# Gate products with the high and low parts of u side by side: wide matmuls, chained products, and a written order for three groups

## The chip, the cores and the metric

The kernel runs on one core of a Trainium2 chip. The time is device time in microseconds of one execution, taken as the median of several runs; the profile is of one execution more. Engines are named as in the profile: PE is TensorE (matmuls), PEld its weight loads, DVE is VectorE, ACT is ScalarE, POOL is GpSimd and SP is SyncE, which issues most of the loads.

## The reference, cut to what matters

One layer of a streaming encoder over 512 frames of 1024 channels: three branches read the normalised input `u`, each branch is projected to 1024 channels, and three sigmoid gates, computed from `u`, merge them.

```python
u = rmsnorm(h, g_mix)
proj = u @ w_in                    # queries, keys, values, ..., 3 gates of 1024 columns
y_gla = o_gla @ w_gla_o            # branch outputs, 512 -> 1024
y_fox = o_fox @ w_fox_o
y_mem = o_mem @ w_mem_o
gt = sigmoid(gates)
merged = gt[0] * y_gla + gt[1] * y_fox + gt[2] * y_mem
h = h + merged @ w_out
u2 = rmsnorm(h, g_ffn)
h = h + square(relu(u2 @ w_ff1)) @ w_ff2
return rmsnorm(h, g_final)
```

All is float32. The change is in the gate products of the memory and the GLA branch, with small moves in the front (where `u` is made) and in the projection by `w_out`.

## The kernel before, in words

**Precision by parts.** Each float32 operand is split into a high part (rounded to the matmul's fp32r format, a cast on ACT) and a low part (the remainder, a subtraction on DVE). A product is three matmuls: high by high, high by low, low by high (`mm3`, L169 to L172). Weights go through `split_w` (L156): the cast is L160, the subtraction L161. Weight tiles rotate through three buffers each for raw, high and low data.

**Gates.** The gate matrix of a branch is 1024 by 1024. It is worked in two groups of 512 output channels (`i` = 0, 1), and each group as a 2 by 2 block product with seven block products instead of eight. On the side of `u` the blocks are quarters (4 channel blocks of 128 by 256 frames) and four sums of quarters (`S1` to `S4`, L1037); `GATE` (L1039) says which of them each of the products 1 to 7 uses. On the side of the weights the sums are made in DRAM order by loads that accumulate: `total` and `other` are loaded (L1064, L1065), and `plus` (L1069, the DMA is L1071, on POOL's queue) adds further blocks to them in place, each time after the split that still needed the earlier sum.

`product` (L1085) computes one block product into one PSUM bank of 2 by 256 columns: 8 pairs of output block `a` and channel block `k`, three matmuls of 256 columns each, 24 in all. `take` (L1094) adds or copies the bank into the four quarters `c11`, `c12`, `c21`, `c22` of the gate (sums at L1080, copies at L1096 and L1101) and applies the sigmoid as a tanh (L1083) when a quarter is complete. `output` (L1118) makes one 128-channel tile of the branch's projection: 12 matmuls of 512 columns (`o_tile`). `merge` (L1125) multiplies gate and projection on DVE (L1127) and adds the result to `acc` on POOL (L1128); for the GLA groups it also splits half of `acc` into `mh`, `ml` (L1131, L1132), the input of the next projection.

There are four groups: memory 0 and 1, GLA 0 and 1. The first has its first two weight tiles ready and makes the sums `S2`, `S4` as it goes (`lefts_2`, L1049). In the three others the order on PE is: products 1 and 2, an output tile, product 5, an output tile, products 3, 6, 7, an output tile, product 4, an output tile.

**Order.** PE's order is as written. On the other engines instructions are put in an order by the framework's scheduler, except where a stretch is wrapped in `in_order` (L138), which chains DVE, ACT and SP in the order of the text, and where `issue_after` puts one instruction behind another. `next_sum` (L122) issues, with each weight cast, one more of the sums of feed-forward weights that are built in DRAM, on POOL's queue.

**Output projection.** `gN` (L184) over `w_out` in two columns of 512 (L1248, L1249). The first column takes the channels two blocks at a time and keeps four banks open; the second loads its four weight tiles first (two of them into own tiles `f0`, `f1`) and goes frame block by frame block. The first two feed-forward weight tiles are split into `f2`, `f3` at L1251.

**Front.** `mem_values` (matmuls at L404) yields 16 steps. Between them stand the sums of squares of x (matmuls at L430), their mean (L431), the power -1/2 on POOL (L432), a transpose that spreads it over partitions (L437), the scaling of x (L441) and the split into `uhi`, `ulo` (L444, L447). `lead_w` (cast L416, subtraction L417) splits weight tiles by hand. The first projection of u starts with the matmuls at L609.

PSUM has eight banks: four named `mm` (products, projections), four named `a` (output tiles, transposes).

## Time and profile before

| what | us |
|---|---|
| median of 3 runs (lowest to highest) | 810.16 (809.69 to 810.54) |
| the profiled execution | 811.06 |
| its span, first instruction to last | 809.3 |
| PE busy in the span | 800.1 |
| DVE, ACT, POOL busy | 595.6, 444.7, 108.0 |
| granted TensorE clock, mean | 0.997 |

Matmuls overlap in the profile, so the time of one matmul in a stream is read from the difference of two starts, not from its duration. The front runs to about 45 us of the span, the first gate group starts near 318, the three others lie between about 346 and 440, the output projection between 440 and 487, and the feed-forward part after it.

### The profile page before, as it was taken

What the parts mean: (1) busy time and instruction counts of PE and PEld (TensorE: products, weight loads), DVE (VectorE), ACT (ScalarE), POOL (GpSimd) and SP (SyncE); (2) the same over time, 40 slices, a digit from 0 to 9 for tenths busy, and PEclk for the clock granted to TensorE, in tenths of its full rate; (3) what the DMA queues carried; (4) which work ended last, traced back from release to release, by engine and by line L of the source; (5) the groups of instructions that cost most, each with busy time, mean ns of one, the idle gap of its engine ahead of it and who ended that gap; (6) DMA issues with size and microseconds to landing.
All of it is one profiled execution on the core that took longest, in us unless ns stands there. A gap on an engine that the chain in (4) does not pass through costs nothing.

```text
span 809.3 us, 12486 instructions
## 1 busy us (share of the span) xinstructions
PE 800.1 (99%) x4799; PEld 704.9 (87%) x4799; DVE 595.6 (74%) x917; ACT 444.7 (55%) x702; POOL 108.0 (13%) x136
## 2 busy tenths in 40 slices
PE   9999999999999999999999999999999999999996
PEld 7788888888888888999999879988998899889985
DVE  6878878456465677877567368897788778877897
ACT  7767555443344234444354347874676367647764
POOL 0001010101101111143144000011001100100011
PEclk9999999999999999999999999999999999999998
DMA  9355665788887867757758723898758966896544
GB/s 358 137 160 175 185 164 178 213 226 246 215 266 239 234 210 198 186 138 206 204 134 238 254 81 130 275 258 217 240 165 195 220 213 173 191 274 202 162 83 130
DMA packets 39628, 161.29 MB, mean 199 GB/s; under 512 B 4752, under 2 KB 5456, under 8 KB 37200
## 3 DMA queue, kind: packets, MB, share of 16 engines
q0 software_dynamic: 9776, 58.20, 34.3%
q1 hardware_dynamic: 28432, 98.34, 34.2%
q10 hardware_dynamic: 1360, 3.96, 1.5%
q8 instruction: 37, 0.61, 0.3%
q14 instruction: 23, 0.19, 0.1%
HBM read 158.35 MB, written 35.68 MB: 240 GB/s over the span
## 4 chain that ended last, share of the span: by engine, by line
PE 94%; DMA 2%; DVE 1%; ACT 1%; issue 0%; POOLq 0%; DVEq 0%; POOL 0%; ACTq 0%
PE mm L1272 20%; PE mm L170 16%; PE mm L171 16%; PE mm L172 16%; PE a L171 5%; PE a L170 5%; PE a L172 5%; DMA raw<-in_wst_dram 2%; PE mm L391 1%; PE a L404 1%; PE a L662 1%; PE a L700 1%; PE a L699 1%; PE a L302 1%; PE a L939 1%; PE mm L618 0%
## 5 line engine op out<-in xcount | busy, mean ns | idle before, releaser
L170 PE MATMUL mm<-uhi,whi 128*128 128x512 f32 (+1 forms) x336 | 119.7, 356 | 0.0
L161 DVE TENSOR_TENSOR wlo<-raw,whi 128x1024 fp32r<-128x1024 f32 x61 | 79.6, 1306 | 53.0 <-ACT whi L160 53.0
L172 PE MATMUL mm<-uhi,wlo 128*128 128x512 f32 (+1 forms) x336 | 117.5, 350 | 0.0
L171 PE MATMUL mm<-ulo,whi 128*128 128x512 f32 (+1 forms) x336 | 117.3, 349 | 0.0
L160 ACT CAST whi<-raw 128x1024 fp32r<-128x1024 f32 x61 | 64.1, 1052 | 84.2 <-PE mm L171 47.8
L1328 ACT CAST hi<-raw 128x1024 fp32r<-128x1024 f32 x52 | 54.4, 1049 | 41.1 <-PE mm L1272 29.5
L1330 DVE TENSOR_TENSOR lo<-raw,hi 128x1024 fp32r<-128x1024 f32 x52 | 63.4, 1223 | 15.7 <-ACT hi L1328 15.7
L170 PEld LDWEIGHTS mm<-uhi,whi 128*128 128x128 f32 x336 | 63.7, 190 | 9.3 <-issue 1.5
L172 PEld LDWEIGHTS mm<-uhi,wlo 128*128 128x128 f32 x336 | 63.6, 189 | 8.5
L171 PEld LDWEIGHTS mm<-ulo,whi 128*128 128x128 f32 x336 | 63.7, 190 | 7.5
L1272 PE MATMUL mm<-u2l,hi 128*128 128x256 f32 x240 | 66.1, 283 | 0.0
L1272 PE MATMUL mm<-u2h,hi 128*128 128x256 f32 x240 | 66.1, 283 | 0.0
L1272 PE MATMUL mm<-u2h,lo 128*128 128x256 f32 x240 | 61.1, 283 | 0.0
L1632 POOL DMA_DIRECT2D b<-in_wst_dram x30 | 25.6, 855 | 262.2 <-DVE lo L1330 136.0
L1272 PE MATMUL mm<-u2sh,hi 128*128 128x256 f32 x192 | 52.5, 283 | 0.0
L1272 PE MATMUL mm<-u2sl,hi 128*128 128x256 f32 x192 | 52.5, 283 | 0.0
L170 PE MATMUL mm<-hi,ch 128*128 128x512 f32 (+1 forms) x132 | 50.9, 386 | 0.0
L171 PE MATMUL mm<-lo,ch 128*128 128x512 f32 (+1 forms) x132 | 50.9, 386 | 0.0
L172 PE MATMUL mm<-hi,cl 128*128 128x512 f32 (+1 forms) x132 | 50.9, 386 | 0.0
L1272 PE MATMUL mm<-u2sh,lo 128*128 128x256 f32 x192 | 47.5, 283 | 0.0
L1272 PEld LDWEIGHTS mm<-u2h,hi 128*128 128x128 f32 x240 | 46.1, 192 | 0.1
L1272 PEld LDWEIGHTS mm<-u2l,hi 128*128 128x128 f32 x240 | 46.1, 192 | 0.1
(446 smaller groups left out, 2144.9 us busy)
## 6 DMA issues: line engine op xcount, KB each, us to landing
raw<-in_wst_dram SPq DMA_DIRECT2D x113, 512.0 KB
raw<-T SPq DMA_DIRECT2D x32, 512.0 KB
b<-in_wst_dram POOLq DMA_DIRECT2D x32, 512.0 KB, 5.5
T<-in_wst_dram POOLq DMA_DIRECT2D x12, 1024.0 KB, 9.0
b<-in_wst_dram SPq DMA_DIRECT2D x16, 512.0 KB
wb<-in_wst_dram POOLq DMA_DIRECT2D x15, 512.0 KB, 5.4
T<-in_wst_dram POOLq DMA_DIRECT2D x12, 512.0 KB, 6.0
wb<-in_wst_dram SPq DMA_DIRECT2D x8, 512.0 KB
```

Source lines behind the costliest of these rows:

```text
L160: cast = nc.scalar.copy(hi, raw)
L161: low_now[0] = nc.vector.tensor_tensor(lo, raw, f(hi), op=ALU.subtract).ins
L170: nc.tensor.matmul(ps, lh, rh, start=start, stop=False, skip_group_check=on)
L171: nc.tensor.matmul(ps, lh, rl, start=False, stop=False, skip_group_check=on)
L172: nc.tensor.matmul(ps, ll, rh, start=False, stop=stop, skip_group_check=on)
L302: nc.tensor.matmul(ps, wz[:, :P], wz, start=True, stop=True)
L391: nc.tensor.matmul(kps[h], w[:, h * P:(h + 1) * P], x[:, k, :], start=k == p == 0, stop=k == KT - 1 and p == 2)
L404: nc.tensor.matmul(ps, x[:, k, sl], w[low][:, kk, :], start=k == low == 0 and x is mxh, stop=k == KT - 1 and low == 1)
L1272: nc.tensor.matmul(ps[:, a, :], x[:, a, k, :], y[:, s, k, :], start=start, stop=stop, skip_group_check=go is not None)
L1328: nc.scalar.copy(hi, raw)
L1330: nc.vector.tensor_tensor(lo, raw, f(hi), op=ALU.subtract)
L1632: nc.gpsimd.dma_start(to[i], wst[index["B", q, i, x]], accum_op=ALU.add)
```

## The change

1. `u` is kept in one tile, high part and low part side by side (`uhl`), and so are the sums (`J1` to `J4`, `own_pair`). A new `product` uses this in three groups: with high weights one matmul reads 256 columns of the high and 256 of the low part and writes both halves of a bank (512 columns); with low weights a matmul of 256 columns goes to the first half. The eight wide ones come first, then the eight narrow ones. A value of the gate is then the sum of the two halves of a bank.
2. Products are chained: a product starts an accumulation (1, 2, 5) or adds to what the bank pair already holds. Products 1, 6, 7, 4 go into the pair `x` and 2, 5, 3 into `y`; the next group swaps the pairs. For this the four `mm` banks become two tiles of two banks (`banks_of`), and the sign of the sums `S2` and of product 6 is turned.
3. The three later groups become a class `Group` whose `run` writes out the order on DVE, ACT and SP (`in_order`). The first group keeps its products.
4. Front: one step of `mem_values` moves from before the sums of squares to after the power, two more go behind the split of u, and one low part of a weight tile waits for the power.
5. Output projection: the first column uses two `a` and two `mm` banks; its weight tiles after the first are split behind the last reads of the gates; the first feed-forward tiles are split behind the last split before them.

The diff, cut to its core:

```diff
-    uhi = up.tile([P, KT, S], F32R, tag="uhi", name="uhi")
-    ulo = up.tile([P, KT, S], F32R, tag="ulo", name="ulo")
+    uhl = up.tile([P, 2, KT, S], F32R, tag="uhl", name="uhl")
+    uhi, ulo = (uhl[:, i] for i in range(2))
...
-        run(islice(mv, 9))
-        lead_w(chunks[7], vraws[1])()
+        run(islice(mv, 8))
+        low = lead_w(chunks[7], vraws[1])
...
-        nc.gpsimd.tensor_tensor(rx, ms, mhalf[:, :NT], op=ALU.pow)
+        power = nc.gpsimd.tensor_tensor(rx, ms, mhalf[:, :NT], op=ALU.pow).ins
+        tc.add_manual_dep(low().ins, power.name, mybir.DependencyInfo(mybir.DependencyClass.Sync, mybir.DependencyReason.DATA),
+                          reason="rest")
         k_copies(range(4))
-        run(islice(mv, 3))
+        run(islice(mv, 2))
...
-        run(islice(mv, 2))
+        run(islice(mv, 4))
...
+        J1, J2, J4 = (op_.tile([P, 2, 4, 256], F32R, tag=f"f{i}", name=nm(f"f{i}")) for i in range(3))
+        J3 = uhl[:, :, 0:4, 256:512]
+        GATE = {1: uhl[:, :, 0:4, 0:256], 2: uhl[:, :, 4:8, 0:256], 4: uhl[:, :, 4:8, 256:512], 5: J1, 6: J2, 3: J4, 7: J3}
...
+            def product(self, n, ps, end=True):
+                wh, wl = (t.rearrange("p (a k c) -> p a k c", a=2, k=4) for t in self.ws[n])
+                for low in range(2):
+                    for a in range(2):
+                        for k in range(4):
+                            to, w, u = (ps[:, a, 0, :], wl, GATE[n][:, 0]) if low else (ps[:, a], wh, GATE[n])
+                            u = u[:, k, :] if low else u[:, :, k, :]
+                            nc.tensor.matmul(to, w[:, a, k, :], u, start=n in (1, 2, 5) and k == low == 0,
+                                             stop=bool(end and low and k == 3), skip_group_check=True)
...
+                self.get("b")
+                self.get(3)
+                self.product(1, x, False)
+                self.plus(self.total, "12")
+                self.plus(self.other, "22")
+                if before:
+                    before.tail()
+                self.high("b")
+                self.low("b")
+                self.get("a")
+                self.product(2, y)
+                if before:
+                    before.merge(before.j)
+                    before.merge(before.j + 1)
+                self.out(j + 2, "b")
+                nc.scalar.copy(c11, y0)
+                vec(c11, c11, y1)
+                self.high(5)
+                self.low(5)
+                self.product(5, y, False)
+                self.plus(self.total, "22")
+                vec(c11, c11, x0)
+                vec(c11, c11, x1)
+                self.high(3)
+                self.tanh(c11)
+                self.low(3)
+                self.out(j + 3, "b")
+                nc.scalar.copy(c22, y0)
+                vec(c22, c22, y1)
+                self.product(3, y)
+                self.high(6)
+                self.low(6)
+                self.high("a")
+                self.low("a")
...
+                self.product(6, x, False)
+                self.plus(self.total, "21")
...
+                self.out(j, "a")
+                nc.scalar.copy(c12, x0)
+                vec(c12, c12, x1)
+                vec(c12, y0, c12, ALU.subtract)
+                vec(c12, c12, y1)
+                self.tanh(c12)
+                self.product(7, x, False)
...
+                self.out(j + 1, "a")
+                self.high(4)
+                vec(c22, c22, x0, ALU.subtract)
+                vec(c22, c22, x1, ALU.subtract)
+                self.tanh(c22)
+                self.low(4)
+                self.product(4, x)
...
+            def tail(self):
+                x = self.pair[0]
+                self.copied = nc.scalar.copy(self.c21, x[:, :, 0, :]).ins
+                self.read = nc.vector.tensor_tensor(self.c21, self.c21, x[:, :, 1, :], op=ALU.add).ins
+                self.tanh(self.c21)
...
+        first_group("gate_mem", "w_mem_o", omh, oml, ready)
+        banks_of(2)
...
+        with in_order():
+            a.run(None, b)
...
+        with in_order():
+            b.run(a, c)
+            c.run(b, None)
+            c.tail()
...
+        column = [at_(), at_(), mmt(), mmt()]
+        run(gN([("N", "w_out", 2 * j, 0) for j in range(4)], of(mh, ml), NT, lambda: column.pop(0), res_evac(0), get=first_w))
...
-        ws = [own_w(("F", 0, 0, b)) for b in ("11", "21")]
+        with tc.issue_after(cast_now[0]), tc.issue_after(low_now[0]):
+            ws = [own_w(("F", 0, 0, b)) for b in ("11", "21")]
```

Here `high` is a cast and `low` a subtraction of one weight tile (each is given its own place now), `get` a load, `out` an output tile, `vec` a sum on DVE, and `tail` the last gate quarter of a group, which is made while the next group's first product runs.

More of the change, by code (lines that the diff above doesn't have):

```diff
@@ L1057, in hybrid_block, with first_group @@
         loaded, summed = [None], [None]
-        def gate_group(gate, wo, oh, ol, i, ready=None, last=None):
+        def first_group(gate, wo, oh, ol, ready):
+            i = 0
             src = {b: wst[index["W", gate, i, b]] for b in ("11", "12", "21", "22")}
@@ L1171, in gate_group @@
             plus(total, "21")
-            if last is not None and i:
-                late_on.append(1)
-            if ready is None:
+            cast, added, low = lefts_2(S4, A12, ALU.add)
+            with tc.issue_after(low):
                 take(6, p6)
-            else:
-                cast, added, low = lefts_2(S4, A12)
-                with tc.issue_after(low):
-                    take(6, p6)
-                output(j)
-                raw = block("22")
-                with tc.issue_after(added):
-                    w = split_w(raw)
-                p3 = product(3, w)
-            take(3, p3)
-            if ready is None:
-                p7 = product(7, split_w(other))
+            output(j)
+            raw = block("22")
+            with tc.issue_after(added):
+                w = split_w(raw)
+            take(3, product(3, w))
             take(7, p7)
@@ L1190, in gate_group @@
             merge(j + 3)
-            if ready is None:
-                output(j)
             with tc.issue_after(cast):
@@ L1202, in hybrid_block @@
+        first_group("gate_mem", "w_mem_o", omh, oml, ready)
+        banks_of(2)
+        pair = [mmt([P, 2, 2, 256]) for _ in range(2)]
+        a = Group("gate_mem", "w_mem_o", omh, oml, 1, pair, 1)
+        a.load()
+        a.begin()
+        b = Group("gate_gla", "w_gla_o", ogh, ogl, 0, pair[::-1], 0)
+        with in_order():
+            a.run(None, b)
         omst.close()
@@ L1214, in hybrid_block @@
             nc.sync.dma_start(gf, gffn)
-        u2 = [up.tile([P, 4, 4, 256], F32R, tag=g, name=n) for g, n in (("uhi", "u2h"), ("ulo", "u2l"))]
+        u2 = up.tile([P, 2, 4, 4, 256], F32R, tag="uhl", name="u2")
+        u2 = [u2[:, i] for i in range(2)]
         mst.close()
@@ L1239, in own_w @@
         def own_w(key):
-            hi, lo = (own_tile(own_n[0] % 4, g) for g in "hl")
+            hi, lo = own_pair(own_n[0] % 4)
             own_n[0] += 1
```

179 lines of the change are left out of this document (127 added, 52 removed).

## The prediction

> **What bounds the kernel now.** I read the page first (busy times, then the chain that ended last), then what TensorE (PE) waited for, then the stretches in which the change lies.
>
> ```profile
> PE 800.1 (99%) x4799; PEld 704.9 (87%) x4799; DVE 595.6 (74%) x917; ACT 444.7 (55%) x702; POOL 108.0 (13%) x136
> PE 94%; DMA 2%; DVE 1%; ACT 1%; issue 0%; POOLq 0%; DVEq 0%; POOL 0%; ACTq 0%
> PE a L302 <- DVE warm L299: 1.2, 1, 1.2
> PE mm L171 <- DVE wlo L161: 1.0, 1, 1.0
> 346.00:377.00 31.00, 31.00 (x217) 29.08 (x216) 21.95 (x22) 13.38 (x16) 11.48 (x10) 1.00 0.72 177
> 377.00:409.00 32.00, 32.00 (x223) 29.88 (x222) 20.51 (x22) 13.80 (x18) 9.63 (x9) 1.00 0.75 190
> 409.00:440.00 31.00, 31.00 (x218) 29.04 (x217) 21.73 (x26) 14.71 (x20) 10.74 (x10) 1.00 0.66 191
> 440.00:470.00 30.00, 29.01 (x128) 23.72 (x127) 16.53 (x19) 12.28 (x18) 6.41 (x6) 1.00 0.80 230
> ```
>
> PE is busy for 99% and is 94% of the chain. It waits twice, 1.2 us at the start and 1.0 us in the output projection. The three stretches of 31 or 32 us (columns: PE, weight loads, VectorE, ScalarE, POOL, granted clock, DMA share, GB/s) are nearly the three gate groups that the change rewrites: there PE never stops, at full granted clock. So in these groups time can come only from PE work that is cheaper, not from a wait that goes; and whatever the new order makes PE wait is added in full.
>
> **The change part by part.** *1. The wide matmuls.* The spacing of matmuls is read from starts in the timeline: one product of 256 columns, one output tile of 512, and a long run of 512.
>
> ```profile
> 326.48 0.28 PE L170 MATMUL mm<-f0h,whi 128*128 128x256 f32 x1
> ...
> 329.35 0.28 PE L170 MATMUL mm<-uhi,whi 128*128 128x256 f32 x1
> ...
> 335.13 0.40 PE L170 MATMUL a<-omh,whi 128*128 128x512 f32 x1
> ...
> 337.88 0.28 PE L170 MATMUL mm<-f2h,whi 128*128 128x256 f32 x1
> ...
> 439.99 0.39 PE L170 MATMUL a<-whi,mh 128*128 128x512 f32 x1
> ...
> 456.77 0.39 PE L172 MATMUL a<-whi,ml 128*128 128x512 f32 x1
> ```
>
> 24 matmuls of a product take 329.35 - 326.48 = 2.87 us, 0.1196 each. Twelve of an output tile take 2.75 us, 0.229 each; the long run does 74 steps in 16.78 us, 0.2268 each. In every product of the three groups eight pairs (high weights by high u, high weights by low u) become eight of 512 columns; the eight with low weights stay at 256. A pair costs 0.239, one of 512 costs 0.227 to 0.229: 0.010 to 0.012 us less. Three groups of seven products hold 168 pairs: 1.7 to 2.1 us. I take **2.0 us**. A product becomes 8 x 0.227 + 8 x 0.120 = 2.78 us.
> The moving operand is now two runs of 256 columns, 4 or 16 KB apart in a partition, which no matmul of the trace reads. Lower bound of the gain: 0, if such a matmul costs as two of 256. Upper: 2.1. I take the row of 512, since the form in columns and bank is the same.
> The two rows give 0.419 ns a column and 12.4 ns fixed for each matmul, and the fixed part is what a pair saves. [...]
>
> *2. What the halves cost elsewhere.* A gate is now the sum of two halves of a bank, so more reads of PSUM.
>
> ```profile
> L1080 DVE TENSOR_TENSOR ct<-ct,mm x24: 674/684/689, 321.6 to 437.4; 128x512 f32<-128x512 f32 x24
> L1096 ACT COPY ct<-mm x4: 570/584/591, 318.9 to 414.3; 128x512 f32<-128x512 f32 x4
> L161 DVE TENSOR_TENSOR wlo<-raw,whi x61: 1212/1225/3097, 44.1 to 465.9; 128x1024 fp32r<-128x1024 f32 x61
> L160 ACT CAST whi<-wb x19: 1032/1049/1056, 319.5 to 429.1; 128x1024 fp32r<-128x1024 f32 x19
> L1128 POOL TENSOR_TENSOR acc<-acc,ct x16: 1284/1600/2286, 345.2 to 442.2; 128x512 f32<-128x512 f32 x16
> 344.27 1.28 DVE L1127 SCALAR_TENSOR_TENSOR ct<-ct,a 128x512 f32<-128x512 f32 x2
> DMA to landing us min/median/max: 5.2/5.4/9.7
> ```
>
> Per group VectorE goes from 7 sums of 0.68 us to 10, ScalarE from 2 copies of 0.58 to 4: 2.1 and 1.2 us more. VectorE had 20.5 to 22 us of 31 to 32, now about 24 of 30.4: hidden under PE, if the order never makes PE wait.
>
> *3. The written order.* In it VectorE, ScalarE and SP take their work strictly in line, so each wait holds all behind it. I laid one group (with a predecessor) out with these durations. Three points come close.
> (a) The next group's first high cast reuses a buffer that is free when the last output tile ends, 2.78 us before that group and 5.56 before its second product, which overwrites the bank pair that the earlier group's last gate is read from. In line: cast 1.05, two low parts 2 x 1.15 (1.23 less overlap), two merges 1.28, the last read 0.68: 5.3 of 5.56, margin 0.25 us.
> (b) The weights of product 6 are summed by a DMA that waits for the low part of product 5. From the end of product 2 to product 6: 2.74 + 2.78 + 2.74 + 2.78 = 11.0 us. The copy and sum of the first gate (1.3), cast 5 and low part 5 end at about 3; behind two accumulations on POOL (the same op took up to 3.1 us beside them) at about 4.2. With landing 5.4 and cast 1.05: 9.5 to 10.7, margin 0.3 to 1.5.
> (c) In the last group product 7 overwrites the banks of 6, and VectorE has two low parts, two halves of the merged sum and the read between: margin about 0.3.
> The two SP loads per output and product are issued as soon as a buffer is free; behind them stand only loads that are due later. ScalarE's and VectorE's extra work is within these sums. I count **+0.2 us** for a small slip; bounds 0 (all margins hold) and 2.1 (0.7 a group, the whole gain).
> The tail copy, sum, tanh, two merges and the split halves after the last group take some 7 us, and the output projection needs channel blocks 4 and 5 only after 48 matmuls of 0.227, 10.9 us: nothing. Its third and fourth column tile use the banks of the last products; the tail has read them 1.6 us after product 4, PE comes there after 12 x 0.227 = 2.7 us: nothing.
>
> *4. The order of splits in the output projection.* The one wait of PE in this region:
>
> ```profile
> 460.43 1.05 ACT L223 CAST f2h<-raw 128x1024 fp32r<-128x1024 f32 x1 [6.88 <-DMA raw<-in_wst_dram]
> 463.12 1.05 ACT L223 CAST f3h<-raw 128x1024 fp32r<-128x1024 f32 x1 [1.64 <-DMA raw<-in_wst_dram]
> 464.08 1.04 ACT L160 CAST whi<-raw 128x1024 fp32r<-128x1024 f32 x1
> 465.83 0.39 PE L170 MATMUL mm<-whi,mh 128*128 128x512 f32 x1
> 465.94 1.22 DVE L161 TENSOR_TENSOR wlo<-raw,whi 128x1024 fp32r<-128x1024 f32 x1
> 467.21 0.50 PE L171 MATMUL mm<-wlo,mh 128*128 128x512 f32 x1 [0.99 <-DVE wlo L161]
> ```
>
> Two splits for the feed-forward part (f2, f3) stood on ScalarE and VectorE ahead of the projection's last weights. The change sends them behind. The last cast needs its buffer, free after three of four steps of the first column (440 + 3 x 5.45 = 456.3), then 1.05 + 1.23: ready at 459, due at 465. So 1.38 becomes 0.23: **-1.15 us**. What comes late next is f2 and f3, first used past 487: covered by 20 us. Bounds: -1.15 and 0.
>
> *5. The front.* One step of four matmuls moves behind the sums of squares, and a low part moves behind the power on POOL.
>
> ```profile
> 22.93 0.40 PE L404 MATMUL a<-hi,mxh 128*128 128x512 f32 x1
> ...
> 23.86 0.95 PE L430 MATMUL a<-ones,xsq 128*128 128x1 f32 x8
> 23.86 1.23 DVE L417 TENSOR_TENSOR lo<-raw,hi 128x1024 fp32r<-128x1024 f32 x1 [0.21 <-ACT hi L416]
> 25.01 0.15 DVE L431 TENSOR_SCALAR ms<-a 128x4 f32<-128x4 f32 x1
> 25.31 1.03 POOL L432 TENSOR_TENSOR rx<-ms,mhalf 128x4 f32<-128x4 f32 x1 [20.62 <-DMA raw<-in_wst_dram]
> 27.25 1.29 DVE L441 TENSOR_TENSOR xt<-xt,a 128x512 f32<-128x512 f32 x2 [2.09 <-PE a L437]
> 31.69 0.61 PE L609 MATMUL mm<-uhi,hi 128*128 128x512 f32 x2
> 32.26 0.73 PE L609 MATMUL mm<-ulo,hi 128*128 128x512 f32 x2
> 32.83 0.39 PE L521 MATMUL mm<-uhi,whi 128*128 128x512 f32 x1
>   DVE ulo L447: 1.2, 3
> ```
>
> The sums start at 22.93 instead of 23.86, 0.93 earlier; mean and power follow, the power ends at about 25.4. The moved low part runs 25.45 to 26.65 on VectorE, and the scaling of x starts there instead of at 27.25: 0.6 us sooner. Behind the low part on VectorE stands exactly that scaling, so the added wait eats 0.3 of the 0.93. PE waits for the low halves of u three times (the weight loads were idle 1.2 us); in matmul starts, four took 32.83 - 31.69 = 1.14 where 4 x 0.227 = 0.91 are due, so 0.23 lost, some 0.7 for three. The head start of 0.6 covers most: **-0.6 us**, bounds -1.2 and 0 (PE does the same steps, later).
>
> *6. Nothing:* the joint tile for high and low u, the changed sign of two sums in the first group, the bank pools (the same eight banks, waits by tile).
>
> Sum: -2.0 + 0.2 - 1.15 - 0.6 = **-3.55 us**. The profiled execution took 811.06 us, with a span of 809.3; it lies 0.9 above the median of the three runs. Against it the sum gives 807.5, against the median of 810.16, **806.6 us**.
>
> **The rivals.**
> *A. The two-run operand streams no faster than two matmuls.* For: no row shows one. Against: columns and bank are those of the 512 rows. 806.6 + 2.0 = 808.6. [...]
> *B. The margins of 0.25 to 0.3 us are not there.* VectorE's low part took 3.1 us once beside POOL; with 0.7 us lost in each of the three groups, the group gain is gone: 806.6 - 0.2 + 2.1 = 808.5. For: two merges and two accumulations now stand in front of the low part of product 5. Against: product 5 first uses low weights 1.8 us after it starts.
> *C. Slower: the summing DMA of point (b) lands late.* ScalarE takes cast 6 in line, so PE, and all casts behind it, wait. It decides from a landing of about 5.7 us; at the longest landing of the row, 9.7, each of the two groups with a predecessor loses 9.7 - 5.7 = 4.0: 806.4 + 8.0 = 814.4. It needs 5.2 us of loss in all to be slower by 0.2%. For: before, cast 6 had more time, because low part 5 ran ahead of the reads. Against: the median landing is 5.4, and the loads on SP are done some 4 us before.
>
> ```profile
> 383.76 0.87 POOL L1071 DMA_DIRECT2D wb<-in_wst_dram  x1 [1.38 <-DVE wlo L161]
> 389.34 1.05 ACT L160 CAST whi<-wb 128x1024 fp32r<-128x1024 f32 x1 [4.17 <-PE mm L172]
> 394.75 0.28 PE L170 MATMUL mm<-f1h,whi 128*128 128x256 f32 x1
> ```
>
> In the second of the three groups the cast ended 4.4 us ahead of product 6 (394.75); by (b) up to 4 of them go.
> *D. More comes:* the whole 1.2 us in front, 2.1 in the groups, no slip: 805.7, and 805.3 if the reordered feed-forward casts help.
>
> **How the numbers follow.** Forecast 0.62 (805.6 to 807.8), A 0.05, A2 0.05, B 0.14, C 0.08, D 0.06. The range reaches from D's 805.3 over A and B to 809.3 and leaves out C and little else. About 0.2%, 1.6 us, is what a measurement tells from no change: faster means below 808.5. Forecast, D, A2 and a little of B (0.01): 0.74; A and the rest of B: 0.18; C: 0.08.
>
> **What would show it.** Step 1: the new products' matmuls of 512 columns start every 0.227 us, a product takes 2.78. Step 3: PE has no idle time in the groups; else a wait for VectorE at the second product or at product 7, or for ScalarE's cast at product 6. Step 4: the wait of 1.0 us for the low weights is gone. Step 5: the scaling of x starts near 26.6. The prediction is wrong if wide matmuls start every 0.24 us or PE waits over 0.5 us in a group.

## The result, and the profile after

The changed kernel takes 826.3 us (median of five runs, 823.7 to 826.7), the kernel before, measured beside it, 810.16: a ratio of 1.0182, 95% interval 1.0169 to 1.0196. I had forecast 806.6. The ratios with their intervals, here and below, come from the runs in the fast state and are not the quotients of the medians; one run of experiment 2 (984.98 us) and one of experiment 4 (1129.91), at a mean clock of 0.752 and 0.655, stand outside them. The profiled execution after took 826.3 us, with a span of 824.2, 14.9 more than before.

I cut both spans at the same points of PE's work: "front" (here all that comes before product 5 of the first gate group, whose products 1 and 2 start near 318), the rest of that group, called the first group below, the three rewritten groups, output projection, feed-forward part. The stretches of the kernel before (columns: length, then busy us of PE, PEld, DVE, ACT, POOL; granted clock, DMA share, GB/s):

```profile
0.00:326.48 326.48, 325.20 (x1755) 271.19 (x1756) 222.17 (x466) 165.16 (x320) 34.22 (x55) 1.00 0.71 212
326.48:346.63 20.15, 20.15 (x145) 18.91 (x144) 17.15 (x19) 10.91 (x13) 3.72 (x5) 1.00 0.72 181
346.63:377.75 31.12, 31.12 (x217) 29.16 (x216) 22.07 (x21) 13.38 (x17) 10.93 (x10) 1.00 0.74 181
...
439.99:487.39 47.40, 46.41 (x217) 38.35 (x216) 26.72 (x38) 20.22 (x35) 8.07 (x9) 1.00 0.56 164
487.39:809.29 321.90, 314.98 (x2039) 288.94 (x2037) 266.00 (x330) 206.60 (x285) 30.76 (x41) 0.99 0.72 196
```

The two groups left out are 31.12 long as well.

The changed kernel:

```profile
0.00:326.91 326.91, 325.15 (x1755) 271.04 (x1756) 222.23 (x466) 165.63 (x320) 35.09 (x56) 1.00 0.70 212
326.91:350.51 23.60, 22.03 (x146) 20.52 (x144) 17.16 (x19) 10.94 (x13) 2.85 (x4) 0.93 0.44 99
350.51:388.02 37.51, 33.21 (x162) 28.36 (x160) 20.20 (x21) 12.90 (x16) 7.32 (x8) 0.91 0.55 138
388.02:423.20 35.18, 32.26 (x162) 27.39 (x161) 20.15 (x24) 13.51 (x17) 8.54 (x9) 0.95 0.58 150
423.20:453.64 30.44, 30.44 (x163) 26.23 (x161) 22.58 (x29) 14.68 (x20) 10.33 (x12) 1.00 0.84 241
453.64:501.45 47.81, 46.72 (x219) 38.33 (x217) 29.78 (x41) 23.17 (x40) 9.04 (x11) 1.00 0.59 177
501.45:824.17 322.72, 315.29 (x2039) 288.88 (x2037) 266.08 (x330) 206.86 (x285) 30.76 (x41) 0.99 0.71 196
```

Length against length: front +0.43, first group +3.45, second +6.39, third +4.06, fourth **-0.68**, output projection +0.41, feed-forward part +0.82. So the last group does what step 1 promised, and three groups lose 13.9 us. In those three PE is busy for less than the stretch and the granted clock is below 1. What PE waited for (us in total, times, longest; these rows give PE's idle time, while the waits in the text are gaps between the starts of two matmuls less the spacing due without a wait, and so 0.1 to 0.2 us longer):

```profile
PE mm L1226 <- ACT whi L1212: 7.2, 2, 4.3
...
PE a L180 <- DVE ml L1249: 1.1, 2, 0.8
PE mm L178 <- ACT whi L168: 0.8, 1, 0.8
PE mm L180 <- DVE wlo L169: 0.8, 1, 0.8
```

The first row is the second and third group: PE waits for the high cast of one weight tile. All its casts but two come in time; the late ones are those of product 6, and each waits on ScalarE for a DMA into `wb`:

```profile
370.45 1.04 ACT L1212 CAST whi<-wb 128x1024 fp32r<-128x1024 f32 x1 [8.09 <-DMA wb<-in_wst_dram]
...
406.62 1.05 ACT L1212 CAST whi<-wb 128x1024 fp32r<-128x1024 f32 x1 [6.71 <-DMA wb<-in_wst_dram]
```

This is the accumulation into `total` that product 6 needs. VectorE has released it long before (low part 5 runs from 357.89 to 359.12).

Why it lands so late stands in POOL's queue, which issues these accumulations:

```profile
360.23 1.75 POOL L1201 DMA_DIRECT2D wb<-in_wst_dram  x2 [2.85 <-DMA wb<-in_wst_dram]
...
397.08 1.75 POOL L1201 DMA_DIRECT2D wb<-in_wst_dram  x2 [1.01 <-DMA wb<-in_wst_dram]
```

"x2" are two issues in line. The first of each pair is the *next* group's block 22 into its `other`; it waits for that group's first loads (2.85 us here; SP issued them only at 353.4 and 353.9). Only behind it comes the sum that the current group is waiting for. It was free to go at 359.1 and went out at 360.8, 1.7 us late. Then it took 9.6 us to land, where the first of the pair took 5.3:

```profile
DMA to landing us min/median/max: 5.3/7.4/9.6
```

So more of the delay comes from landing second than from the place in line. In the third group the pair went at 397.08, landed after 5.9 and 8.9 us, and the cast began at 406.62. In the fourth group, which has no successor, the sum goes alone, 5.6 us before its cast begins, and nothing waits. In the kernel before, the urgent sum goes first (354.44), and the next group's only in the pair at 362.38, as its second:

```profile
354.44 0.86 POOL L1071 DMA_DIRECT2D wb<-in_wst_dram  x1
362.38 1.73 POOL L1071 DMA_DIRECT2D wb<-in_wst_dram  x2 [7.07 <-DVE wlo L161]
```

After the wait there is a second loss. Product 6 runs from 371.55 to 376.84 and from 407.71 to 412.18, 5.29 and 4.47 us instead of 2.78, PE busy throughout. The two stretches, by the columns above, show it at a granted clock of 0.50 and 0.62:

```profile
371.55:376.84 5.29, 5.29 (x16) 4.52 (x17) 3.48 (x3) 1.85 (x2) 0.86 (x1) 0.50 0.43 63
...
407.71:412.18 4.47, 4.46 (x17) 3.69 (x17) 3.48 (x3) 1.85 (x2) 0.86 (x1) 0.62 0.34 39
```

In the first group the next group's sum (320.81) holds nothing up in line, since its load had long landed. It is under way beside the first group's own: the one issued at 324.19 lands after 8.4 us (5.3 for the one at 324.02 in the kernel before). PE waits twice for it, 0.97 and 0.92 us, first for the cast and then for the low part behind it, and here too slow matmuls follow:

```profile
336.19:339.60 3.41, 3.41 (x17) 3.31 (x16) 3.41 (x4) 1.06 (x1) 0.00 (x0) 0.50 0.81 132
```

Matmuls of 256 columns start every 0.21 us in it instead of 0.12; the stretch costs about 1.6 us.

So 6.39 in the second group is 4.46 of wait + 2.51 slow product + 0.1 of slow matmuls after it - 0.68 gain; 4.06 in the third is, to 0.02, 3.07 + 1.69 - 0.68.

### The profile page after: what moved, and what is told of

Read it like the earlier page. It is cut to its first block, busy times and chain, and to the rows that moved or that the text cites. A ratio compares the mean times of both kernels' runs of the same rounds, so it can differ in the third digit from the quotient of the medians.

```text
span 824.2 us, 12146 instructions
## 1 busy us (share of the span) xinstructions
PE 805.1 (98%) x4631; PEld 700.8 (85%) x4631; DVE 598.2 (73%) x926; ACT 447.7 (54%) x708; POOL 103.9 (13%) x136
## 4 chain that ended last, share of the span: by engine, by line
PE 45%; DMA 5%; ACT 2%; DVE 2%; issue 1%; POOL 0%; SPq 0%; POOLq 0%; DVEq 0%; ACTq 0%
PE mm L1450 18%; PE mm L1226 5%; PE mm L179 4%; PE mm L180 4%; PE mm L178 4%; DMA wb<-in_wst_dram 3%; PE a L180 3%; PE a L178 3%; PE a L179 3%; DMA b<-in_wst_dram 1%; ACT hi L1561 1%; DMA raw<-in_wst_dram 1%; PE a L1435 0%; ACT whi L1212 0%; DVE lo L1565 0%
## 5 line engine op out<-in xcount | busy, mean ns | idle before, releaser
L169 DVE TENSOR_TENSOR wlo<-raw,whi 128x1024 fp32r<-128x1024 f32 x49 | 59.8, 1222 | 50.7 <-ACT whi L168 50.5
L178 PE MATMUL mm<-uhl,whi 128*128 128x512 f32 (+1 forms) x240 | 92.5, 386 | 0.0
L180 PE MATMUL mm<-uhl,wlo 128*128 128x512 f32 (+1 forms) x240 | 90.4, 377 | 0.0
L179 PE MATMUL mm<-uhl,whi 128*128 128x512 f32 (+1 forms) x240 | 90.1, 376 | 0.0
L1450 PE MATMUL mm<-u,hi 128*128 128x256 f32 x480 | 82.2, 283 | 0.0
L1450 PEld LDWEIGHTS mm<-u,hi 128*128 128x128 f32 x480 | 72.0, 192 | 0.2
L1450 PE MATMUL mm<-u,lo 128*128 128x256 f32 x240 | 61.1, 283 | 0.0
L178 PEld LDWEIGHTS mm<-uhl,whi 128*128 128x128 f32 x240 | 45.3, 189 | 9.0 <-issue 1.5
L180 PEld LDWEIGHTS mm<-uhl,wlo 128*128 128x128 f32 x240 | 45.2, 188 | 8.6
L179 PEld LDWEIGHTS mm<-uhl,whi 128*128 128x128 f32 x240 | 45.3, 189 | 7.3
L1450 PEld LDWEIGHTS mm<-u,lo 128*128 128x128 f32 x240 | 43.0, 192 | 0.0
L1506 ACT CAST hi<-b 128x1024 fp32r<-128x1024 f32 x26 | 27.3, 1050 | 27.9 <-PE mm L180 21.4
```

What stands on the lines that cost most here:

```text
L169: low_now[0] = nc.vector.tensor_tensor(lo, raw, f(hi), op=ALU.subtract).ins
L178: nc.tensor.matmul(ps, lh, rh, start=start, stop=False, skip_group_check=on)
L179: nc.tensor.matmul(ps, lh, rl, start=False, stop=False, skip_group_check=on)
L180: nc.tensor.matmul(ps, ll, rh, start=False, stop=stop, skip_group_check=on)
L1450: nc.tensor.matmul(ps[:, a, :], x[:, a, k, :], y[:, s, k, :], start=start, stop=stop, skip_group_check=go is not None)
L1506: nc.scalar.copy(hi, raw)
```

## The experiments

All times are compared with runs of the kernel before made beside them. My main theory: the order of POOL's queue makes the sums late, and half-rate matmuls follow each wait. Rivals: the margins of the written order on VectorE, ScalarE and SP are too small; or the wide matmuls are the trouble.

**1. POOL's sums in text order.**

```diff
             def plus(self, to, b):
-                nc.gpsimd.dma_start(to, self.src[b], accum_op=ALU.add)
+                with tc.issue_after(summed[0]):
+                    summed[0] = nc.gpsimd.dma_start(to, self.src[b], accum_op=ALU.add).ins
```

> The changed kernel, with the four accumulating weight loads of each of the three later groups chained on POOL's queue in the order of the text (as the kernel before had them). Main theory: the loss comes from POOL's queue, where the next group's accumulation stood ahead of the one that product 6 waits for, and from the slow matmuls that follow each wait. Then the waits of 4.5 us (second group) and 3.1 us (third), the slow product 6 behind each and the two waits in the first group go; of the 14.9 us, 3.45 + 6.4 + 4.06 = 13.9 go, and the group part of the gain stays: 826.3 - 13.9 = 812.4, and about 811 if the three groups then each gain the 0.67 us that the last one showed (2 x 0.67 more). Product 6 follows product 3 without a wait, PE's clock is granted in full. Rival 1 (the margins of the written order are too small: VectorE, ScalarE and SP taken in line make PE wait): order on POOL changes little, the waits for the cast of product 6 stay above 2 us each, 820 or more. Rival 2 (the wide matmuls themselves throttle the clock): product 6 stays at half rate also without a wait, 818 or more.

Measured 814.53 us; ratio 1.0046 (1.0034 to 1.0057). By the ratios the one edit takes the loss from 14.7 us to 3.7. The waits of the first group and of the second are gone. But 811 was expected, and PE still waits: for the cast of product 6 in two groups, for the last halves in the projection, for a low part in the feed-forward part.

The sums for product 6 now go alone. POOL's timeline of this kernel, one issue for each group:

```profile
356.07 0.87 POOL L1202 DMA_DIRECT2D wb<-in_wst_dram  x1 [1.39 <-DVE wlo L1218]
...
386.76 0.87 POOL L1202 DMA_DIRECT2D wb<-in_wst_dram  x1 [1.38 <-DVE wlo L1218]
...
417.76 0.87 POOL L1202 DMA_DIRECT2D wb<-in_wst_dram  x1 [1.38 <-DVE wlo L1218]
```

ScalarE's timeline, the cast behind each:

```profile
361.50 1.05 ACT L1213 CAST whi<-wb 128x1024 fp32r<-128x1024 f32 x1 [2.72 <-DMA wb<-in_wst_dram]
...
393.28 1.05 ACT L1213 CAST whi<-wb 128x1024 fp32r<-128x1024 f32 x1 [4.07 <-DMA wb<-in_wst_dram]
...
426.07 1.04 ACT L1213 CAST whi<-wb 128x1024 fp32r<-128x1024 f32 x1 [5.87 <-DMA wb<-in_wst_dram]
```

From issue to cast 5.4, 6.5 and 8.3 us, in the second, third and fourth group; PE waits 0, 0.44 and 2.24 us. The fourth group is clean in the changed kernel. The loads for the residual stand beside it here (SP's timeline), but at the same distance ahead of its sum as there:

```profile
408.82 1.10 SPq L1382 DMA_DIRECT2D h<-in_xN_dram  x2
```

They went out 8.9 us before the sum in this kernel, and 9.0 in the changed one (423.71 and 432.67). What is new is one more accumulation. The group's block 22 into `other`, which the swap had sent out a group earlier (397.08), now stands in a pair at the group's start, where the changed kernel has a single issue:

```profile
407.57 1.74 POOL L1202 DMA_DIRECT2D wb<-in_wst_dram  x2 [10.83 <-DVE wlo L1218]
```

```profile
422.47 0.85 POOL L1201 DMA_DIRECT2D wb<-in_wst_dram  x1 [12.40 <-DVE wlo L1217]
```

The second of that pair lands only after 11.9 us, at 420, while the sum for product 6 is under way. Experiment 5 takes the loads away and leaves the pair, and the wait goes too: the wait needed both. The theory holds for what it named; the remainder needed another: transfers that run at the same time stretch the landing (issue to cast 8.3 us here, 5.3 in experiment 5).

**2. Narrow matmuls in that kernel.** Each wide matmul becomes two:

```diff
-    nc.tensor.matmul(ps[:, a], w[:, a, k, :], GATE[n][:, :, k, :], ...)
+    for g in range(2):
+        nc.tensor.matmul(ps[:, a, g, :], w[:, a, k, :], GATE[n][:, g, k, :], ...)
```

> As the kernel with POOL's sums in text order, but each wide matmul of 512 columns made as two of 256, one into each half of the bank (same chaining of products, same reads, same order). By step 1 of the prediction a pair costs 0.239 us and a wide one 0.227: three groups of 56 pairs lose 2.0 us (1.7 to 2.1) against that kernel; a group lasts 0.67 us longer. [...]

In this one the start flag stands on both halves of a bank, and it leaves out a part of its sums (experiment 8, with one start flag a bank, has them all); the instructions are the same in number and size. Measured 814.68 us, ratio 1.005 (1.0037 to 1.0063): no difference, as rival A said, and for another reason. Its PE waits 1.9 us less in all; the time that the wide form saves is spent waiting for the same sums. It says nothing yet on the form itself; experiment 8 does.

**3. The old front in that kernel** (the three edits of the front undone).

```diff
-        run(islice(mv, 8))
-        low = lead_w(chunks[7], vraws[1])
+        run(islice(mv, 9))
+        lead_w(chunks[7], vraws[1])()
...
```

> As the kernel with POOL's sums in text order, but with the front as before the change (the step of the memory values ahead of the sums of squares, the low part not behind the power). By what the profile after shows (the first gate group starts 0.43 us later than before the change) the old front is 0.4 us faster; by step 5 of the prediction it is 0.6 us slower.

Measured 814.9 us, ratio 1.0054 (1.0042 to 1.0066), against 1.0046 (1.0034 to 1.0057): no difference that can be told. In the profiles product 5 of the first group starts between 326.3 and 327.2 with the new front, and at 326.48, 326.82 and 326.93 with the old one: the scatter covers it. This run has something else to show. In its fourth group PE waits 2.26 us, in experiment 1 it waited 2.24, and the clock behind the two differs. The stretch of product 6 in this kernel, columns as above:

```profile
427.40:431.87 4.47, 4.47 (x17) 3.77 (x17) 4.47 (x5) 2.89 (x4) 1.89 (x3) 0.62 0.35 41
```

And in that of experiment 1:

```profile
427.17:430.07 2.90, 2.90 (x16) 2.55 (x17) 2.90 (x4) 2.90 (x4) 1.09 (x2) 1.00 0.00 0
```

4.47 us at 0.62 of the clock, and 2.90 us at 1.00. What the runs show of such waits is set side by side in the last section.

**4. The kernel before without its chain on POOL.**

```diff
             def plus(to, b):
-                with tc.issue_after(before) if before is not None else ExitStack():
+                with ExitStack():
                     summed[0] = ...
```

> The kernel before, with one thing taken away: its accumulating weight loads are no longer put behind those of the earlier group on POOL's queue, so that a load of the next group can stand ahead of one that the current group waits for, as in the changed kernel. No wide matmul, no written order, old front. Main theory: PE waits for casts behind late accumulations in each group that has a successor, 3 to 6 us each with the slow matmuls behind it: 816 to 828. Rivals (the written order on VectorE, ScalarE and SP, or the wide matmuls, are what costs): no change, 810 to 811.

Measured 815.44 us, ratio 1.0054 (1.0039 to 1.0068): by the ratio 4.4 us slower with neither wide matmul nor written order. Size and place differ from what I expected: nearly all of it is in the first group (23.9 us instead of 20.15), and the clock stays at 1.00. POOL's timeline has the swapped pair in one row, behind its wait:

```profile
333.15 1.74 POOL L1071 DMA_DIRECT2D wb<-in_wst_dram  x2 [8.10 <-DMA wb<-in_wst_dram]
```

The 8.1 us of that wait cost nothing: the urgent sum, the second of the pair, was free at 333.7 and went out at 334.0. But as the second it landed after 8.9 us, where in the kernel before it goes first (332.64) and lands after 5.3, and PE waits for its cast and low part. So the missing chain costs by itself, through the landing. The one later sum that runs ahead of its group (374.64) went alone, with no urgent sum behind it.

**5. The residual's loads later,** on the kernel of experiment 1: the five loads go behind the third and fourth weight load of the projection.

```diff
-        with tc.issue_after(loaded[0]):
-            for t in range(NT):
-                nc.sync.dma_start(hN[t], xN[t * P:(t + 1) * P, :])
...
         def first_w(key):
...
+            with tc.issue_after(d):
+                if key[2] == 4:
+                    h_loads((0, 1))
+                    nc.sync.dma_start(gf, gffn)
+                if key[2] == 6:
+                    h_loads((2, 3))
```

> The kernel with POOL's sums in text order (814.5 us), with the five loads of 512 KB for the residual (four tiles h and the gain gf) moved on SP's queue behind the third and fourth weight load of the output projection; they had started at 408.8 to 410, while the sum for product 6 of the last group was on its way (it landed after 8.25 us and PE waited 2.24 us; beside fewer loads it landed after 5.4 and 6.5 us). Theory: the rest of the loss is this landing under shared DMA bandwidth; it falls to about 6 us, the wait of 2.24 us goes: 812.3. Rival (the landing is long because of POOL's own two sums in flight and the sums for the feed-forward weights on the same queue): no change, 814.5.

Measured 812.25 us, ratio 1.0022 (1.0006 to 1.0037). The sum is issued and landed in 5.3 us, and the wait of 2.24 is gone. It goes out at 417.65, and ScalarE's cast follows:

```profile
422.99 1.05 ACT L1213 CAST whi<-wb 128x1024 fp32r<-128x1024 f32 x1 [2.91 <-DMA wb<-in_wst_dram]
```

**6. The last halves of the merged sum first,** on the kernel of experiment 1: the fourth weight tile of the projection and those of its second column are split behind the last `mh`, `ml`.

```diff
...
-            with tc.issue_after(c.read), tc.issue_after(c.copied):
+            late_split = (c.half, c.rest) if key[2] == 6 else (c.read, c.copied)
+            with tc.issue_after(late_split[0]), tc.issue_after(late_split[1]):
                 return split_w(raw)
```

> The kernel with POOL's sums in text order (814.5 us), with the last halves of the merged sum (the last two mh, ml) ahead of the later weight casts of the output projection on ScalarE and VectorE. In that kernel the two stood behind a cast that waited 3.5 us for its load, and PE waited 0.58 and 0.94 us for them. Theory: both waits go: 813.0. Rival (the weight cast that now stands behind is late in its place): a wait for the weights of the fourth step takes their place, 814 to 815.

Measured 812.87 us, ratio 1.0019 (1.0009 to 1.0029). PE's waits in the projection are gone and none takes their place. In the changed kernel the halves stood behind casts that waited for loads. Its ScalarE timeline: the first row waits 3.41 us for a load, and the two halves (`mh`, the first of them in the second row) come behind it in line:

```profile
461.30 1.06 ACT L168 CAST whi<-raw 128x1024 fp32r<-128x1024 f32 x1 [3.41 <-DMA raw<-in_wst_dram]
...
463.48 0.62 ACT L1248 ACTIVATE mh<-acc 128x512 fp32r<-128x512 f32 x1
```

**7. Both edits,** those of experiments 5 and 6.

> Both edits, loads for the residual later and halves first, on the kernel with POOL's sums in text order: 814.5 - 2.2 - 1.5 = 810.8, what is left of PE's waits then being 0.4 us in the third group and 0.9 us in the feed-forward part. If the two causes are not independent (the late load of the weights is itself due to the loads for the residual), the sum is less than the two alone.

Measured 809.66 us, ratio 0.9977 (0.9967 to 0.9987). The spans of the profiled runs add up: 812.5, with one edit 810.0 and 810.1, with both 807.9. By the medians the edits alone give 2.3 and 1.7 us and both together 4.9; the runs with one edit scatter over 4 to 6 us. So nothing shows that one cause hangs on the other, and that the gains simply add is shown only to about 1 us.

**8. Both edits, narrow matmuls** (the edit of experiment 2, with one start flag a bank).

> As the kernel with both edits, but each wide matmul of 512 columns made as two of 256. Where the earlier pair of kernels showed no difference because PE waited for the sums anyway, here PE has few waits left: by step 1 of the prediction 2.0 us slower than the wide form; if product 6 still waits in the groups, as much less as these waits shrink (0.4 us or so): 1.6 to 2.0.

Measured 810.24 us, ratio 0.9989 (0.998 to 0.9997), 0.6 us more in the whole time. The three groups alone, as one stretch of this kernel:

```profile
346.46:439.89 93.43, 93.43 (x649) 87.49 (x648) 63.26 (x72) 41.26 (x53) 27.40 (x27) 1.00 0.71 187
```

And of experiment 7:

```profile
347.25:439.25 92.00, 91.53 (x481) 78.69 (x480) 64.16 (x72) 41.30 (x53) 27.33 (x27) 1.00 0.71 189
```

1.43 us, though the wide form has a wait of 0.63 us in it (at product 6 of the third group): 2.06 net. The rest of the difference is lost outside: up to the end of the first group the profiled run of experiment 7 is 0.8 us longer (same code), and the feed-forward part gives 0.6 back.

**9. The next group's loads behind cast 6,** on the kernel of experiment 7: `load` makes its first DMA wait for that cast, and the second follows in line.

```diff
-                    after.load()
+                    after.load(cast6)
```

> The kernel with POOL's sums in text order, the residual's loads later and the halves first (809.66 us), with one edit more: the next group's two first loads wait for the cast of product 6, so that they do not share the DMA engines with the accumulation for it. In that kernel they were issued at 378.2 and 378.6 in the third group and moved between 385 and 389, while the accumulation issued at 387.1 landed after 6.5 us and PE waited 0.63 us. Theory (landing is stretched by loads that run beside it): it lands after about 5.4 us, the wait goes: 809.0. Rival (6.5 us is the accumulation's own, behind the two earlier ones of the group): no change, 809.7.

Measured 810.97 us, ratio 0.9997 (0.9988 to 1.0006), where experiment 7 had 0.9977: worse. The profiled run, at 809.68 us, is among the fastest. The wait at product 6 went as the theory said (issue 387.14, cast 392.49: 5.35 us), but the held loads, with three more behind them in SP's line, went out at 393.6 to 396.3, and the next accumulation, issued in the middle of them, took 10.1 us; PE waited 1.5 us at product 4. POOL's second issue:

```profile
395.10 0.85 POOL L1205 DMA_DIRECT2D wb<-in_wst_dram  x1 [7.09 <-DVE wlo L1221]
```

And the cast behind it on ScalarE:

```profile
405.18 1.04 ACT L1216 CAST whi<-wb 128x1024 fp32r<-128x1024 f32 x1 [5.06 <-DMA wb<-in_wst_dram]
```

**10. Matmuls in place of the waits,** in the changed kernel as it is.

```diff
...
+                if after:
+                    self.busy(j, 14 if before else 20)
                 self.product(6, x, False)
```

> The changed kernel as it is (826.3 us, POOL's sums not in text order), with matmuls added on PE in front of product 6: 20 of 512 columns in the second group, 14 in the third, on data at hand, into a bank that the next output tile overwrites; they fill the waits of 4.5 and 3.1 us. Theory (the half-rate matmuls of product 6 come from PE's idle time before them): product 6 takes 2.78 us instead of 5.29 and 4.47, so 2.5 + 1.7 us less: 822.1. Rival (the half rate has another cause, such as the work itself or the load on memory): product 6 stays at half rate, 826.3 or a little more.

Measured 819.73 us (819.15 to 822.06), ratio 1.0108 (1.0094 to 1.0122); the profiled execution took 822.06. Product 6 is at full rate behind the fill: 370.29 to 373.06, 2.77 us, where the changed kernel took 5.29; in the third group 2.90. PE's timeline of this kernel, product 6 and the matmul behind it:

```profile
370.29 1.98 PE L1226 MATMUL mm<-f,whi 128*128 128x512 f32 x8
...
373.06 0.40 PE L178 MATMUL a<-omh,whi 128*128 128x512 f32 x1
```

By its starts of products the second group is 2.6 us shorter than in the changed kernel and the third 1.3, where 2.5 and 1.7 were expected. Another 1.7 us lie in the first group, which has no filler: PE waits twice there too (0.65 and 0.92 us), and this time no half rate follows. More work on PE, and a faster kernel: without the idle time before product 6 there is no half rate behind it. Why the median lies another 2.3 us below the profiled execution I did not follow up.

**11. Loads behind cast 6, narrow matmuls.**

> As the kernel with the next group's loads held back (all mended), but each wide matmul of 512 columns made as two of 256. With no wait left in the groups, step 1 of the prediction gives 2.0 us slower than the wide form (1.7 to 2.1) at the start of the output projection; the whole time may show less where the feed-forward part behind waits for something else.

Measured 811.76 us, ratio 1.0004 (0.9994 to 1.0013): 0.8 us above experiment 9, not 2.0, since 9 has the new wait of 1.5 us and this kernel, being slower, has only 0.26 us of it (in the second group).

**12. Only the second of the two loads later,** behind the low part of the projection's weights that follows cast 6, on the kernel of experiment 7: here `load` makes only its second DMA wait.

```diff
-                    after.load()
+                    after.load(low_a)
```

> The kernel with POOL's sums in text order, the residual's loads later and the halves first (809.66 us); of the next group's two first loads only the second (whose sum is due 20 us later) waits, for the low part of the tile that follows cast 6. Holding both back took the wait at product 6 away (landing 5.35 us) and gave a new one of 1.5 us at product 4 in the third group, whose accumulation then landed behind five held loads. Theory (accumulations are late in proportion to the loads in flight when they are issued): with 0.5 MB less beside each of the two accumulations neither waits, 809.0. Rival (the held load and the ones behind it in line on SP again run ahead of the accumulation for product 4): a wait of up to 1.5 us there, 809.7 to 810.5.

Measured 808.91 us, ratio 0.9978 (0.9968 to 0.9988): faster than the changed kernel and, by 1.8 us (1.0 to 2.6), than the kernel before. By its ratio it cannot be told from experiment 7 (0.9977); what the edit does is seen in the waits. PE waits for nothing in the groups and in the projection. Its stretches, cut as above, with the three later groups as one:

```profile
0.00:326.57 326.57, 325.17 (x1756) 271.11 (x1756) 222.06 (x466) 165.86 (x321) 34.22 (x55) 1.00 0.70 212
326.57:346.73 20.16, 20.16 (x146) 18.91 (x144) 17.14 (x19) 10.34 (x13) 2.82 (x4) 1.00 0.44 102
346.73:438.00 91.27, 91.27 (x481) 78.65 (x480) 64.20 (x72) 41.25 (x53) 27.30 (x27) 1.00 0.72 191
438.00:484.13 46.13, 46.13 (x218) 38.45 (x217) 29.23 (x41) 23.63 (x40) 8.87 (x11) 1.00 0.65 202
484.13:806.91 322.78, 315.27 (x2039) 288.86 (x2037) 265.85 (x330) 206.37 (x285) 30.75 (x41) 1.00 0.72 196
```

## Why the prediction was wrong, step by step

**Step 1, the wide matmuls: right.** The three groups together take 91.27 us in the last kernel, 93.36 before (three times 31.12): -2.09, where -2.0 was counted. A product takes 2.77 to 2.79 us. Wide against narrow in one kernel (experiments 7 and 8) is 2.06, which is 12.3 ns a pair. Rival A falls, and so does a smaller saving, to which I had given 0.05 as A2: no run shows one.

**Step 2, the reads of PSUM: right,** hidden in every run: in experiment 12 VectorE is busy for 64.20 us of the 91.27 of the three groups, and PE waits for nothing in them.

**Step 3, the written order: wrong, and this is the step that failed.** The point was the right one, (b), and so was what PE would wait for: the cast of product 6 behind its summing DMA. That is rival C, at 0.08. The layout of (b) held as well: low part 5 ended 3.06 us after product 2, where about 3 was counted. The reason for the wait was another. I put the landing at its median of 5.4 us with a margin of 0.3 to 1.5 and asked what orders VectorE, ScalarE and SP. I did not ask what orders POOL. `in_order` chains three engines, POOL is not among them; the old `plus` stood behind the earlier group's sums by `issue_after`, and the new `plus` in the diff has lost it. The framework then put the next group's sum first, and the urgent one landed second. The price of that stood in the row that I had read: its longest landing, 9.7 us, is the second of the pair at 362.38, the next group's sum, for which nobody was waiting; the first of that pair took 5.4. So the loss fell not on the groups with a predecessor, but on those with a successor, the first group among them, for which I had counted nothing. The term of +0.2 (bounds 0 and 2.1) was 15.3: the first three groups are 13.9 longer, with the 1.4 that step 1 gains in two of them already in that. About 9.4 of it are waits; the other 5.9 are matmuls at half rate behind the waits, a term that I did not have at all.

With the order restored (experiment 1) margin (b) itself proved too small as well: beside other transfers issue to cast is 6.5 and 8.3 us, not 5.4. Margins (a) and (c) held: no run shows a wait at the second product or at product 7.

"The tail ... nothing" for the output projection was wrong by 1.4 us. I added up 7 us of work against 10.9 and left out that weight casts not held back by anything may stand in the middle of it, and wait there for loads (3.41 us in the changed kernel).

**Step 4, the order of splits in the projection: right.** The old wait is gone in all runs with that change; in the changed kernel the tail's two waits hid it. Without them the projection takes 46.13 us against 47.40: -1.27, where -1.15 was counted.

**Step 5, the front: a part, and not to be seen in the whole.** -0.6 was counted. The scaling of x does start at 26.72 in the changed kernel, before at 27.25. At 45 us, where the front proper ends, the same matmul starts at 44.92 to 45.25 with the new front and at 45.24 to 45.69 with the old. From there to product 5 of the first group PE takes 281.2 to 282.0 us whichever front it is, which covers so little: in the last kernel that product starts at 326.57, before at 326.48, and experiment 3 shows no difference. Some profiles show the reason for a part: PE waits for the squares of x before the sums, so the head start of 0.93 is not all to be had (0.2 us in experiments 5 and 7).

**The sum.** In the best version -2.09 and -1.27 are there, +0.09 in front and +0.88 in the feed-forward part (322.78 against 321.90): span -2.4 where the prediction had -3.55. In the feed-forward part PE waits for a low part on VectorE, by 0.2 to 0.9 us; in experiments 5 and 6 it does, in 8 and 9, which reach that part within 1 us of them, not at all. What decides it stays open.

## What to carry to other kernels

When a change rewrites a helper that issues DMAs, list every queue that it issues to, POOL's too, and ask for each what holds its order now. An accumulation put ahead of an urgent one cost twice here: by its own wait (the urgent one went out 1.7 us late), and by landing first (after 5.3 us, the urgent one after 9.6). Price a wait of PE with the slow matmuls that may follow: here 2.51 us behind a wait of 4.46, and 1.69 behind 3.07. Making PE faster moves it towards the DMAs: where it then waits for a landing the gain does not show (experiments 1 and 2, 814.53 and 814.68 us), so measure the landing beside the loads that will run at that time (up to 8.3 us in experiment 1), not its median (5.4).

## What the runs showed of the hardware

- **The clock after a wait.** The length of a wait alone does not settle it: half rate came after 3.1 and 4.5 us, after 2.26 (experiment 3) and not after 2.24 (experiment 1), after two waits of 0.97 and 0.92 and not after two of 1.7 and 0.9 (experiment 4). In the changed kernel the granted clock is 0.50 from 336.19 on for 3.41 us (the row is in the section on the result), from 370.32 for 6.83 and from 407.87 for 3.41, and once more from 820.88 to the end, behind the last matmul. The first three begin 34.13 and 37.55 us apart, 10 and 11 times 3.41:

```profile
370.32:377.15 6.83, 5.60 (x17) 4.83 (x18) 3.50 (x3) 3.01 (x4) 0.86 (x1) 0.50 0.38 59
407.87:411.28 3.41, 3.41 (x9) 2.63 (x10) 3.32 (x3) 1.69 (x2) 0.86 (x1) 0.50 0.26 29
820.88:824.17 3.29, 0.00 (x0) 0.00 (x0) 0.00 (x0) 0.00 (x0) 0.00 (x0) 0.50 0.35 135
```

  In the 3.41 us just before each of the first three the clock is 1.00 and PE is busy for 1.85, 0.34 and 0.50 us:

```profile
332.77:336.19 3.42, 1.85 (x14) 1.48 (x13) 2.46 (x3) 2.83 (x3) 0.86 (x1) 1.00 0.01 2
366.91:370.32 3.41, 0.34 (x3) 0.14 (x2) 0.00 (x0) 0.00 (x0) 0.00 (x0) 1.00 0.74 149
404.45:407.87 3.42, 0.50 (x4) 0.29 (x4) 0.17 (x1) 1.25 (x2) 0.00 (x0) 1.00 0.45 131
```

  In experiment 3 it is 1.31 us in the row that ends inside product 6 (from 427.40 on, at 0.62 of the clock):

```profile
424.44:427.85 3.41, 1.31 (x10) 1.07 (x9) 0.47 (x1) 1.55 (x2) 0.00 (x0) 1.00 0.31 123
```

  That the half rate hangs on PE's idle time is shown by experiment 10: with matmuls in place of the wait product 6 takes 2.77 us, not 5.29. Why the wait of 2.24 us in experiment 1 passed without it is not shown; that it counts where a wait falls, and not its length alone, is my guess from these few cases, in which the ends of matmuls are modelled.
- **An accumulating DMA of 512 KB** took 5.3 us from issue to the cast behind it where an edit had moved loads away from it (experiments 5 and 9), and 5.4, 6.5 and 8.3 in the three later groups of experiment 1, beside other transfers; 10.1 beside the five held loads of experiment 9. Of two issued in line (at 332.64, 362.38 and 391.95 in the kernel before, 360.23 and 397.08 in the changed one) the first landed after 5.3 to 5.9 us, the second after 8.3 to 9.7; the second of the pair took 8.9 in experiment 4 and 11.9 in experiment 1.
- **Two runs of 256 columns in one matmul** start every 0.226 us, like one run of 512 in the kernel before (0.227 to 0.229): eight take 1.81 us from places 4 KB apart (370.29 to 372.10 in experiment 10) and 1.81 from places 16 KB apart (346.73 to 348.54 in experiment 12).
